# Retention's value and key projections moved from the middle stage's end to beside the sparse attention's lower half

## The chip, the core and the metric

The kernel runs on one core of a Trainium2 chip. The metric is the device time of one execution in microseconds (us). Matrix products run on TensorE (PE; its loads of weights are shown as PEld), the rest on VectorE (DVE), ScalarE (ACT) and GpSimd (POOL); SyncE (SP) issues nearly all transfers (DMAs). Each engine takes its instructions in the order in which the program has them, and waits at one until its inputs and its output buffer are ready.

## What is computed

One layer of a decoder over 1024 positions of width 1024: an RMS norm, one input projection into all the parts below, three groups of heads, a gate, one output projection with the residual, and a last RMS norm. Cut to what matters:

```python
u = rms_norm(h, attn_norm[layer])
proj = jnp.einsum('bsd,dc->bsc', u, w_in[layer])
(dq, dk, dv, sq, ckv, iq, ik, iw, rq, rk, rv, gate) = jnp.split(proj, split_points, axis=-1)
o_a = diff_attention(dq, dk, dv, ...)                        # 6 heads, dense causal, two maps each
o_b = dsa_attention(sq, rms_norm(ckv, ...), iq, ik, iw, ...) # 6 heads, the 256 best keys of each query
o_c = retention(rotary(rq, ...), rotary(rk, ...), rv, ...)   # 4 heads, chunks of 128 with a state
y = jax.nn.silu(gate) * jnp.concatenate([o_a, o_b, o_c], axis=-1)
h = h + jnp.einsum('bsc,cd->bsd', y, w_out[layer])
```

## The kernel before

Positions are worked in 8 blocks of 128. Float32 products of high precision are made of three matmuls, with each operand split into a high part and the small rest (`split`, L121): the names ending in `h` and `l`, as `wh` and `wl`, are these.

**Units of the input projection.** `gemm` (L269) makes one unit. The raw weights `wr` come from HBM through a ring of two buffers (`rtile`, L228) and are split by POOL into tiles `wh` and `wl` of a pool of five (`wsplit`, L242). A unit of retention (`rq`, `rk`, `rv`, 256 columns) has 8 tiles of 128 positions; each is 24 matmuls (L282 to L284) into a PSUM tile `pG`, of which there are two. `ret_evac` (L469) takes such a tile to SBUF: for `rv` one ACT copy (L479), for `rq` and `rk` two products on DVE (L491, L492) and three POOL instructions (L494 to L498). The result lies in a tile `rt` of a pool of three (`hl`) until its store to the DRAM array `rd` (L499), an SP transfer.

**Attention.** `attend` (L585) is used by both attentions. One step is one block of queries of one head: scores into PSUM `pS` (for the sparse one L720 and L721), scores with the mask to a tile `pp` with the row's maximum (DVE, L728), exponential (ACT, L729), normalization (DVE, L734 and L736), transposes into `pB` (L611), their copies to `pt` (ACT L113, or L115 where the scheduler may choose), and after each pair of blocks the product with the values `v` (L626). The sparse attention's lower half, `dsa(p, 0)`, takes blocks 0 to 3 against up to 512 keys, the upper half, `dsa(p, 1)`, blocks 4 to 7 against up to 1024; each has 3 pairs of heads, so 24 steps. Its output is multiplied with the gate (L758) and stored (L763).

**Stages.** `run` (L831) issues the work in stages. `interleave` (L58) draws from several generators and takes next the one whose issued cost, divided by its weight, is smallest. The middle stage mixes the dense attention, the selection of keys (`topk`, `ties`) and a list of projection units, `order` and the part of `order2` ahead of the bar, at weight `wg`. Then the values of the sparse attention are loaded (`v_load`, L811). The next stage mixes the sparse attention's lower half, the last `ties`, and, at weight `gw`, the units behind the bar followed by retention's first half with `out_weights` and the first part of block 7's output projection. The last mix is the sparse attention's upper half with retention's second half (blocks 4 to 7) and the output projection of two blocks. The output projection (`project`, L905) of the other blocks ends the program.

`out_weights` (L894) loads the output weights in 16 pieces through the same two `wr` buffers. For each of 8 row groups one piece is copied by ACT into `woh` (L113) with its rest `wol` by DVE (L123), the other is done by POOL alone (L119, L123). `woh` and `wol` take the place of the split input `uh` and `ul`, so the first waits for the last projection matmul.

The stages set the order in which instructions are issued to the framework. A scheduler then orders each engine's queue by its own timeline, so that instructions of neighbouring stages mix.

```python
interleave((seq(*(self.diff(p) for p in range(3))), K["wd"]),
           (seq(self.topk(), self.ties((3, 2))), K["wt"]),
           (units(K["order"] + " " + K["order2"].split("|")[0]), K["wg"]))
self.v_load()
interleave((seq(*(self.dsa(p, 0) for p in range(3))), 100), (self.ties((7, 6, 5, 4)), 110),
           (seq(units(K["order2"].split("|")[1]), mix((self.retention(0), K["rw"]),
                        (seq(self.out_weights(), self.project(K["pp"], 0)), K["ow"]))), K["gw"]))
```

Of the kernel before, what the change touches and what calls it, by code (L numbers as in the profile page):

```python
# [28 lines left out]
    0, 384, 768, 1152, 1536, 1664, 2176, 2248, 2504, 2760, 3016)  # L29
WA = 384 + 72  # L30
C_R = (C_RQ, C_RK, C_RV)
K = {'mk': 'up ky', 'mp': 's2 g5 g4', 'rt': ('hl', 'pq'), 's0': ('gg', 'gg', 'ag', 'gg', 'vg', 'gg', 'vg', 'vg'), 'xp': 2, 'bufs': (8, 3, 3, 5, 3, 4, 1), 'pp': (7,), 'rot': 0, 'order': 'g0 g1 k1 q1 k2', 'order2': 'q2 g2 rq g6 s0 ck g7 s1 M g3 rv rk | ', 'wd': 36, 'wt': 13, 'wg': 119, 'gw': 56, 'rw': 26, 'rx': 132, 'pw': 40, 'ow': 84, 'nf': 2, 'ev': 200, 'late': 8, 'de': ('aa', 'aa', 'aa'), 'da': 'ax', 'gd': (7, 4, 2), 'hlp': 'sqkk', 'tkp': '', 'vt': 'v', 'rs': 'x', 'nv': 1, 'dn': 'v', 'ws': 'gg', 'oe': ('av', 'gg'), 'one': 0, 'idx': (42, 40), 'iqs': 'iq2 iq3 q0 k0'}
NST, NP, NPQ, NW, NHL, NHALF, NY = K["bufs"]


# [33 lines left out]
class Trunk:  # L69
# [65 lines left out]
    def setup(self):  # L135
# [8 lines left out]
        for b in range(NB):  # L144
            self.x[b] = self.slot("x", [128, 1024])
            nc.sync.dma_start(self.x[b], i["x"][0, b * 128:(b + 1) * 128, :])
            if b == K["xp"] - 1:
                self.wide()
# [93 lines left out]
    def wsplit(self, c0, w):  # L242
        hs, ls = [], []
        if w == WA:
# [5 lines left out]
            for k in range(KC):  # L250
                self.split(hs[k], ls[k], self.dvw[k // 2][:, k % 2], *K["s0"][k])
            return hs, ls
        n = 1024 // w
        for k0 in range(0, KC, n):
            h, l = (self.wtile("w" + x, [n, w]) for x in "hl")
            for j in range(0, n, n // 2):
                raw = self.rtile([n // 2, w])
                self.nc.sync.dma_start(raw, self.i["w_in"][0, (k0 + j) * 128:(k0 + j + n // 2) * 128,
                                                           c0:c0 + w].rearrange("(k p) c -> p k c", p=128))
                self.split(h[:, j:j + n // 2], l[:, j:j + n // 2], raw, *K["ws"])  # L260
            hs += [h[:, j] for j in range(n)]
# [3 lines left out]
    def evict(self, evac, *args):  # L265
        with self.tc.high_priority(offset=K["ev"]):
            evac(*args)
# [21 lines left out]
    def to_dram(self, key, n=2):  # L289
# [3 lines left out]
        def evac(half, ps):  # L293
            sl = slice(half * 512, half * 512 + 512)
            t = self.sb.tile([128, 2, 512], FR, name=self.name("hl"), tag="hl", bufs=NHL)
            if key[:2] in K["hlp"]:
                nc = self.nc
# [682 lines left out]
```

## Time and profile before

| | |
|---|---|
| median of the runs shown | 781.14 us |
| the three runs | 777.98, 781.14, 785.86 us |
| the profiled execution | 785.29 us |
| its span, first to last instruction | 783.6 us |
| busy in the span: PE, DVE, ACT, POOL | 724.2, 551.5, 447.6, 311.5 us |
| mean granted clock of TensorE | 0.974 |
| moved by DMA | 113.05 MB |

Stretches of the trace are named by the time from the span's start. The span lies 1.7 us below the profiled execution's own time; that execution is 4.15 us slower than the median. Busy time of PE counts each matmul from its start to its modelled end, and matmuls overlap: how many fit is read from the distance between the starts. The idle time before an instruction, with what ended it, stands in brackets behind it; the name after the arrow is the engine, tile and line that was waited for. The granted clock is a share of full speed: 1.0 is the level of 2.4 GHz and 0.5 that of 1.2 GHz, and a value between them is a mean over a stretch with both.

### The profile page before, as it was taken

What the parts mean: (1) busy time and instruction counts of PE and PEld (TensorE: products, weight loads), DVE (VectorE), ACT (ScalarE), POOL (GpSimd) and SP (SyncE); (2) the same over time, 40 slices, a digit from 0 to 9 for tenths busy, and PEclk for the clock granted to TensorE, in tenths of its full rate; (3) what the DMA queues carried; (4) which work ended last, traced back from release to release, by engine and by line L of the source; (5) the groups of instructions that cost most, each with busy time, mean ns of one, the idle gap of its engine ahead of it and who ended that gap; (6) DMA issues with size and microseconds to landing.
All of it is one profiled execution on the core that took longest, in us unless ns stands there. A gap on an engine that the chain in (4) does not pass through costs nothing.

```text
span 783.6 us, 12891 instructions
## 1 busy us (share of the span) xinstructions
PE 724.2 (92%) x4314; PEld 597.4 (76%) x4314; DVE 551.5 (70%) x1312; ACT 447.6 (57%) x989; POOL 311.5 (40%) x343
## 2 busy tenths in 40 slices
PE   3999999999999999988799789998978999999996
PEld 3798888887887898766577567997855887787884
DVE  5920277789999989999889997325657766664443
ACT  4531255559888968787755566434356656554332
POOL 6401322225434438557347699335733242120000
PEclk9999999999999999999899999999968999999999
DMA  9303645454374352461274476564578974413351
GB/s 332 78 1 71 197 136 145 139 137 132 99 218 115 85 163 78 120 169 35 67 206 144 144 215 190 158 192 160 158 213 236 281 200 127 123 48 108 118 176 59
DMA packets 93250, 113.05 MB, mean 144 GB/s; under 512 B 11904, under 2 KB 63488, under 8 KB 93056
## 3 DMA queue, kind: packets, MB, share of 16 engines
q1 hardware_dynamic: 91888, 109.61, 48.1%
q10 hardware_dynamic: 1296, 2.62, 0.9%
q8 instruction: 34, 0.56, 0.3%
q14 instruction: 32, 0.26, 0.1%
HBM read 75.50 MB, written 36.18 MB: 143 GB/s over the span
## 4 chain that ended last, share of the span: by engine, by line
PE 61%; DVE 16%; DMA 6%; issue 6%; POOL 5%; ACT 4%; SPq 0%; DVEq 0%; POOLq 0%; ACTq 0%
PE pB L626 6%; PE pG L130 6%; PE pG L132 6%; PE pG L131 5%; PE pB L611 4%; PE pG L282 4%; PE pG L936 4%; PE pG L937 4%; PE pG L935 4%; PE pG L283 4%; PE pG L284 4%; DVE jv L378 3%; DMA wr<-in_w_in_dram 2%; PE pS L344 2%; PE pS L343 2%
## 5 line engine op out<-in xcount | busy, mean ns | idle before, releaser
L130 PE MATMUL pG<-uh,wh 128*128 128x512 f32 x352 | 141.6, 402 | 1.8 <-DVE gt L827 1.8
L132 PE MATMUL pG<-uh,wl 128*128 128x512 f32 x352 | 140.7, 400 | 0.6 <-POOL wl L123 0.6
L131 PE MATMUL pG<-ul,wh 128*128 128x512 f32 x352 | 139.4, 396 | 0.0
L123 POOL TENSOR_TENSOR wl<-wr,wh 128x512 fp32r<-128x512 f32 x56 | 79.3, 1430 | 106.3 <-PE pG L131 69.4
L392 ACT ACTIVATE ja<-sc,tk_c 128x896 int8<-128x896 f32 (+2 forms) x93 | 83.2, 895 | 17.3 <-DVE tk_c L399 12.0
L113 ACT ACTIVATE pt<-pB 128x512 f32<-128x512 f32 (+2 forms) x120 | 58.8, 496 | 43.8 <-PE pB L611 43.5
L130 PEld LDWEIGHTS pG<-uh,wh 128*128 128x128 f32 x352 | 66.8, 190 | 16.4 <-DVE gt L827 2.4
L132 PEld LDWEIGHTS pG<-uh,wl 128*128 128x128 f32 x352 | 66.4, 189 | 16.1 <-POOL wl L123 0.9
L611 PE MATMUL pB<-ident,pp 128*128 128x128 f32 x432 | 72.9, 287 | 5.5 <-DVE gt L758 3.4
L626 PE MATMUL pB<-pt,v 128*64 128x128 f32 x864 | 70.8, 302 | 7.6 <-ACT pt L113 7.0
L131 PEld LDWEIGHTS pG<-ul,wh 128*128 128x128 f32 x352 | 66.7, 189 | 13.0 <-issue 0.2
L626 PEld LDWEIGHTS pB<-pt,v 128*64 128x64 f32 x864 | 57.7, 147 | 18.9 <-ACT pt L113 9.5
L378 DVE TENSOR_SCALAR_CACHE_REDUCE jv<-sc,tk_c 128x640 bf16<-128x640 f32 (+4 forms) x81 | 69.2, 855 | 1.0
L611 PEld LDWEIGHTS pB<-ident,pp 128*128 128x128 f32 x432 | 51.2, 144 | 22.2 <-issue 9.1
L677 POOL TENSOR_SCALAR pq<-pq,mx 128x896 f32<-128x896 f32 (+7 forms) x48 | 43.2, 901 | 58.6 <-DVE mx L676 55.8
L119 POOL TENSOR_SCALAR wh<-wr 128x512 fp32r<-128x512 f32 x56 | 37.8, 680 | 59.9 <-DMA wr<-in_w_in_dram 54.3
L282 PE MATMUL pG<-wh,uh 128*128 128x256 f32 x192 | 55.0, 288 | 2.6 <-POOL wh L119 2.6
L283 PE MATMUL pG<-wl,uh 128*128 128x256 f32 x192 | 54.9, 286 | 0.0
L284 PE MATMUL pG<-wh,ul 128*128 128x256 f32 x192 | 54.3, 284 | 0.0
L346 ACT ACTIVATE pp<-pS 128x1024 f32<-128x1024 f32 (+5 forms) x48 | 36.5, 760 | 31.1 <-PE pS L344 31.0
L651 PE MATMUL pS<-st,st 128*128 128x512 f32 (+3 forms) x144 | 43.3, 368 | 11.5 <-DVE mx L662 8.9
L351 DVE SCALAR_TENSOR_TENSOR sc<-pp,iw,sc 128x1024 f32<-128x1024 f32 (+5 forms) x42 | 43.5, 1044 | 14.3 <-ACT pp L346 13.6
(218 smaller groups left out, 1756.1 us busy)
## 6 DMA issues: line engine op xcount, KB each, us to landing
wr<-in_w_in_dram SPq DMA_DIRECT2D x56, 256.0 KB, 3.2
st<-qdq SPq DMA_DIRECT2D x24, 256.0 KB, 4.2
st<-qkk SPq DMA_DIRECT2D x18, 256.0 KB, 5.9
x<-in_x_dram SPq DMA_DIRECT2D x8, 512.0 KB, 6.6
qiq<-hl SPq DMA_DIRECT2D x16, 256.0 KB, 3.5
st<-qiq SPq DMA_DIRECT2D x8, 512.0 KB, 3.3
wr<-in_w_out_dram SPq DMA_DIRECT2D x16, 256.0 KB, 3.4
xr<-in_x_dram SPq DMA_DIRECT2D x8, 512.0 KB, 3.5
```

The source lines that it names most:

```text
L113: self.nc.scalar.activation(out, in_, AF.Copy)
L123: (self.nc.vector if e2 == "v" else self.nc.gpsimd).tensor_tensor(lo, src, hi.bitcast(F), OP.subtract)
L130: mm(ps, wh, xh, start=start, stop=False)
L131: mm(ps, wh, xl, start=False, stop=False)
L132: mm(ps, wl, xh, start=False, stop=stop)
L282: mm(ps, uh, hs[k], start=k == 0, stop=False)
L283: mm(ps, uh, ls[k], start=False, stop=False)
L284: mm(ps, ul, hs[k], start=False, stop=k == KC - 1)
L378: nc.vector.tensor_scalar(jv[:, :nv[b]], hb if b == 7 and bit >= 16 else sc[b], t, 0.0, op0=op, op1=OP.add, accum_out=cnt[:, j:j + 1])
L392: nc.scalar.activation(ja[:, :nv[b]], sc[b], AF.Sign, bias=cut(b), scale=-1.0, accum_out=cnt[:, cols[b]:cols[b] + 1])
L611: nc.tensor.transpose(p[:, k], pr[:, (k0 + k) * 128:(k0 + k + 1) * 128], self.ident)
L626: self.last = nc.tensor.matmul(o[u * 64:(u + 1) * 64], vals[k], pts[g, a][:, k, u * 128:(u + 1) * 128], start=k == (i if u else 0), stop=k ...
```

## The change

Two entries of the table `K` that steers the program. The units `rv` and `rk` move behind the bar of `order2`, from the middle stage into the stage with the sparse attention's lower half; the weight `gw` of that stage's third stream rises from 56 to 97, which keeps about the former pace of issue for what follows the two units. The weights of the middle stage stay as they are.

```diff
-'order2': 'q2 g2 rq g6 s0 ck g7 s1 M g3 rv rk | '
+'order2': 'q2 g2 rq g6 s0 ck g7 s1 M g3 | rv rk'
...
-'gw': 56
+'gw': 97
```

No instruction is added or taken away. The orders of the engines are alike up to the first matmul of `rv`; `ties` keep their places on DVE, with other buffer numbers alone.

On PE, the sparse attention's first scores before: `pS900` is its first tile of scores, `pG847` and `pG851` are tiles of `rv`, `pB844` and `pB850` are values and transposes of the dense attention.

```order
L284 MATMUL pG847_4929<-wh813_4728,ul_106 128x256
L720 MATMUL pS900_5637<-st898_5631,st899_5632 128x384
L626 MATMUL pB844_4905<-pt833_4859,v46_294 64x128 x7
L611 MATMUL pB850_4958<-ident_70,pp837_4874 128x128
L282 MATMUL pG851_4966<-wh809_4718,uh_105 128x256
```

On PE, the sparse attention's first scores in the changed order: `pS852` is that first tile of scores, `pG882` and `pG915` are the second and the third tile of `rv`, `pB816` and `pB821` belong to the dense attention.

```order
L284 MATMUL pG882_5236<-wh862_5144,ul_106 128x256
L626 MATMUL pB816_4744<-pt803_4696,v46_294 64x128 x11
L611 MATMUL pB821_4771<-ident_70,pp808_4715 128x128 x3
L720 MATMUL pS852_5117<-st850_5111,st851_5112 128x384
L721 MATMUL pS852_5117<-st850_5111,st851_5112 128x384
L282 MATMUL pG915_5380<-wh858_5134,uh_105 128x256
```

The first scores stand behind the fourth tile of `rv` before, and behind the second now; before, the second half of them (L721) follows only behind the eighth.

On PE, from the last projection matmul on, before: `pG889` is the last tile of `rk`, `pS971`, `pS977` are scores, `pB956` and `pB963` values, the other `pB` transposes, all of the sparse attention's lower half.

```order
L284 MATMUL pG889_5371<-wh871_5128,ul_106 128x256
L626 MATMUL pB956_5839<-pt948_5812,v897_5629 64x128 x3
L611 MATMUL pB961_5863<-ident_70,pp951_5821 128x128
L720 MATMUL pS971_5903<-st966_5890,st967_5891 128x512
L721 MATMUL pS971_5903<-st966_5890,st967_5891 128x512
L720 MATMUL pS977_5922<-st966_5890,st967_5891 128x128
L721 MATMUL pS977_5922<-st966_5890,st967_5891 128x128
L611 MATMUL pB962_5868<-ident_70,pp955_5836 128x128 x2
L626 MATMUL pB963_5872<-pt960_5862,v897_5629 64x128 x3
L611 MATMUL pB979_5926<-ident_70,pp970_5900 128x128 x3
```

On PE, from the last projection matmul on, in the changed order: `pG1051` is the last tile of `rk`, `pS983` and `pS988` are scores, `pB970` values, the other `pB` transposes, and `pG1055` is retention's first block.

```order
L284 MATMUL pG1051_6180<-wh1033_5946,ul_106 128x256
L611 MATMUL pB967_5622<-ident_70,pp956_5566 128x128 x4
L720 MATMUL pS983_5713<-st978_5694,st979_5695 128x512
L721 MATMUL pS983_5713<-st978_5694,st979_5695 128x512
L626 MATMUL pB970_5634<-pt962_5604,v849_5109 64x128 x7
L611 MATMUL pB975_5663<-ident_70,pp965_5613 128x128
L720 MATMUL pS988_5735<-st978_5694,st979_5695 128x128
L721 MATMUL pS988_5735<-st978_5694,st979_5695 128x128
L611 MATMUL pB976_5671<-ident_70,pp969_5631 128x128 x2
L522 MATMUL pG1055_6217<-ident_70,rt1053_6214 128x128
```

Before, `pS971` is the tenth of the lower half's 24 score tiles, and scores of 15 steps stand behind the last projection matmul; now `pS983` is the eighteenth, and 7 stand behind it.

On ACT, from the seventh to the eighth copy of output weights, before: `woh` are the copies, `pp` exponentials of the sparse attention's upper half, `pt` copies of transposes, `yh` the split of block 7's projection input, `rt` retention's first block.

```order
L113 ACTIVATE woh_5720<-wr1024_6111 128x512
L113 ACTIVATE pt1076_6301<-pB1078_6310 128x2x128
L729 ACTIVATE pp1114_6517,mx1113_6516<-pp1114_6517,mx1113_6516 128x1024
L113 ACTIVATE yh1068_6264<-yr1066_6260 128x384
L729 ACTIVATE pp1126_6553,mx1125_6552<-pp1126_6553,mx1125_6552 128x640
L113 ACTIVATE pt1122_6538<-pB1123_6539 128x4x128
L115 COPY pt1122_6538<-pB1124_6545 128x3x128
L443 ACTIVATE rt907_5657<-rt907_5657 128x256
L444 ACTIVATE rt907_5657<-rt907_5657 128x256
L729 ACTIVATE pp1131_6579,mx1130_6578<-pp1131_6579,mx1130_6578 128x768
L113 ACTIVATE pt1122_6538<-pB1128_6564 128x4x128
L113 ACTIVATE woh_5720<-wr1053_6212 128x512
```

On ACT, from the sixth to the eighth copy, in the changed order, with the same names.

```order
L113 ACTIVATE woh_6224<-wr1068_6277 128x512
L113 ACTIVATE pt1140_6628<-pB1141_6629 128x4x128
L115 COPY pt1140_6628<-pB1142_6635 128x128
L113 ACTIVATE pt1140_6628<-pB1146_6649 128x4x128
L113 ACTIVATE woh_6224<-wr1070_6285 128x512
L115 COPY pt1140_6628<-pB1147_6655 128x2x128
L729 ACTIVATE pp1149_6662,mx1148_6661<-pp1149_6662,mx1148_6661 128x1024
L729 ACTIVATE pp1157_6715,mx1156_6714<-pp1157_6715,mx1156_6714 128x640
L113 ACTIVATE pt1153_6700<-pB1154_6701 128x4x128
L115 COPY pt1153_6700<-pB1155_6707 128x3x128
L113 ACTIVATE woh_6224<-wr1073_6300 128x512
```

Between the last two copies stood three exponentials of the upper half, and now two; between the sixth and the seventh stand none now. Counted over the whole queue, four exponentials of the upper half stood ahead of the eighth copy, and seven do now. The exponentials between successive copies, from the first to the eighth, are now 3, 2 and 3 of the lower half, then 2, 3, 0 and 2 of the upper.

## Rows read from the trace of the kernel before

**Rows 1.** The page, busy us (share of the span) and instructions of each engine.
```profile
PE 724.2 (92%) x4314; PEld 597.4 (76%) x4314; DVE 551.5 (70%) x1312; ACT 447.6 (57%) x989; POOL 311.5 (40%) x343
```

**Rows 2.** Stages: length; busy PE, PEld, DVE, ACT, POOL (count); clock; DMA share; GB/s.
```profile
484.00:559.50 75.50, 72.75 (x589) 66.52 (x589) 31.18 (x94) 27.85 (x74) 38.07 (x51) 1.00 0.54 167
559.50:609.30 49.80, 41.47 (x247) 29.97 (x247) 34.09 (x104) 27.93 (x72) 19.35 (x22) 0.83 0.79 221
609.30:724.70 115.40, 112.83 (x880) 91.70 (x878) 71.77 (x161) 65.72 (x142) 26.01 (x36) 1.00 0.49 144
724.70:783.60 58.90, 51.48 (x222) 41.80 (x222) 23.80 (x54) 17.60 (x42) 0.00 (x0) 0.97 0.34 118
```

**Rows 3.** PE in order of time, projection of retention: start, us, instruction.
```profile
523.22 0.28 PE L282 MATMUL pG<-wh,uh 128*128 128x256 f32 x1
523.34 0.28 PE L283 MATMUL pG<-wl,uh 128*128 128x256 f32 x1
```

**Rows 4.** PE in order of time, steps of the sparse attention between projections.
```profile
533.97 1.09 PE L626 MATMUL pB<-pt,v 128*64 128x128 f32 x14
534.99 0.33 PE L611 MATMUL pB<-ident,pp 128*128 128x128 f32 x1
...
539.18 0.65 PE L626 MATMUL pB<-pt,v 128*64 128x128 f32 x6
539.76 0.55 PE L611 MATMUL pB<-ident,pp 128*128 128x128 f32 x3
540.06 0.42 PE L720 MATMUL pS<-st,st 128*128 128x384 f32 x1
...
540.50 0.28 PE L282 MATMUL pG<-wh,uh 128*128 128x256 f32 x1
```

**Rows 5.** ACT in order of time, four of the eight copies of output weights.
```profile
572.84 0.63 ACT L113 ACTIVATE woh<-wr 128x512 fp32r<-128x512 f32 x1 [3.10 <-DMA wr<-in_w_out_dram]
...
578.01 0.63 ACT L113 ACTIVATE woh<-wr 128x512 fp32r<-128x512 f32 x1 [1.50 <-DMA wr<-in_w_out_dram]
...
597.69 0.62 ACT L113 ACTIVATE woh<-wr 128x512 fp32r<-128x512 f32 x1
...
609.33 0.63 ACT L113 ACTIVATE woh<-wr 128x512 fp32r<-128x512 f32 x1 [2.40 <-DMA wr<-in_w_out_dram]
```

**Rows 6.** Tile wr, 555 to 615 us: durations (ns, min/median/max), first and last start, waits.
```profile
L113 ACT ACTIVATE woh<-wr x8: 616/629/631, 559.4 to 609.3; 128x512 fp32r<-128x512 f32 x8
...
L123 DVE TENSOR_TENSOR wol<-wr,woh x8: 672/689/1540, 560.5 to 610.0; 128x512 fp32r<-128x512 f32 x8
...
  ACT woh L113: 7.0, 3
...
DMA to landing us min/median/max: 2.9/3.4/7.3
```

**Rows 7.** PE in order of time, the wait between the projections of values and keys.
```profile
532.00 0.51 PE L282 MATMUL pG<-wh,uh 128*128 128x256 f32 x2 [2.56 <-POOL wh L119]
```

**Rows 8.** ACT in order of time, first and fourth exponential of the upper half.
```profile
595.93 1.04 ACT L729 ACTIVATE pp<-pp,mx 128x896 f32<-128x896 f32 x1 [0.41 <-DVE mx L728]
...
605.41 0.94 ACT L729 ACTIVATE pp<-pp,mx 128x768 f32<-128x768 f32 x1
```

**Rows 9.** Two stretches of stage 2, columns as in rows 2.
```profile
573.40:594.90 21.50, 18.23 (x82) 12.44 (x82) 13.20 (x46) 11.58 (x33) 8.15 (x8) 0.60 0.72 206
594.90:602.50 7.60, 5.71 (x40) 4.06 (x40) 5.12 (x14) 4.68 (x11) 0.00 (x0) 1.00 0.86 254
```

**Rows 10.** PE in order of time, where the first of these stretches begins.
```profile
574.45 0.66 PE L611 MATMUL pB<-ident,pp 128*128 128x128 f32 x4 [3.38 <-DVE gt L758]
...
576.38 1.97 PE L626 MATMUL pB<-pt,v 128*64 128x128 f32 x14
```

**Rows 11.** PE in order of time, output projection alone.
```profile
724.94 0.39 PE L936 MATMUL pG<-wol,yh 128*128 128x512 f32 x1
725.17 0.40 PE L937 MATMUL pG<-woh,yr 128*128 128x512 f32 x1
```

More of the change, by code (lines that the diff above doesn't have):

```diff
@@ L31 @@
 C_R = (C_RQ, C_RK, C_RV)
-K = {'mk': 'up ky', 'mp': 's2 g5 g4', 'rt': ('hl', 'pq'), 's0': ('gg', 'gg', 'ag', 'gg', 'vg', 'gg', 'vg', 'vg'), 'xp': 2, 'bufs': (8, 3, 3, 5, 3, 4, 1), 'pp': (7,), 'rot': 0, 'order': 'g0 g1 k1 q1 k2', 'order2': 'q2 g2 rq g6 s0 ck g7 s1 M g3 rv rk | ', 'wd': 36, 'wt': 13, 'wg': 119, 'gw': 56, 'rw': 26, 'rx': 132, 'pw': 40, 'ow': 84, 'nf': 2, 'ev': 200, 'late': 8, 'de': ('aa', 'aa', 'aa'), 'da': 'ax', 'gd': (7, 4, 2), 'hlp': 'sqkk', 'tkp': '', 'vt': 'v', 'rs': 'x', 'nv': 1, 'dn': 'v', 'ws': 'gg', 'oe': ('av', 'gg'), 'one': 0, 'idx': (42, 40), 'iqs': 'iq2 iq3 q0 k0'}
+K = {'mk': 'up ky', 'mp': 's2 g5 g4', 'rt': ('hl', 'pq'), 's0': ('gg', 'gg', 'ag', 'gg', 'vg', 'gg', 'vg', 'vg'), 'xp': 2, 'bufs': (8, 3, 3, 5, 3, 4, 1), 'pp': (7,), 'rot': 0, 'order': 'g0 g1 k1 q1 k2', 'order2': 'q2 g2 rq g6 s0 ck g7 s1 M g3 | rv rk', 'wd': 36, 'wt': 13, 'wg': 119, 'gw': 97, 'rw': 26, 'rx': 132, 'pw': 40, 'ow': 84, 'nf': 2, 'ev': 200, 'late': 8, 'de': ('aa', 'aa', 'aa'), 'da': 'ax', 'gd': (7, 4, 2), 'hlp': 'sqkk', 'tkp': '', 'vt': 'v', 'rs': 'x', 'nv': 1, 'dn': 'v', 'ws': 'gg', 'oe': ('av', 'gg'), 'one': 0, 'idx': (42, 40), 'iqs': 'iq2 iq3 q0 k0'}
 NST, NP, NPQ, NW, NHL, NHALF, NY = K["bufs"]
```

## The prediction

> **What bounds the kernel now.** I read the page first, then the busy time by stages, then the instructions of TensorE (PE) and ScalarE (ACT) in order of time. The page has PE busy for 92% of the span [rows 1]; VectorE (DVE) follows at 70%. I cut the end of the kernel into four stages [rows 2]. Stage 1 (484.0 to 559.5 us) holds the projections of the retention's values and keys; stage 2 (559.5 to 609.3) begins with their last matmul and ends with the eighth and last ACT copy of the output weights; stage 3 (609.3 to 724.7) is the rest of the sparse attention's upper half with retention and output projection; stage 4 is output projection alone. Stages 1, 3 and 4 are PE's: busy 72.75 of 75.5, 112.83 of 115.4, and dense to the last projection matmul. Stage 2 is the weak one: PE 41.47 of 49.8 at a mean clock of 0.83, DVE 34.09, ACT 27.93. No engine fills it.
>
> How full PE is depends on the row that one trusts. By matmul busy time stage 2 has 8.3 us free. The loads of weights, PEld, are busy 29.97 us of it, which leaves 19.8 us [rows 2]. The Trainium skill (Perfetto Trace Analysis, Identifying the Most-Contended Engine) says that matmul busy time misjudges TensorE and that the share of weight loads should be used. The trace agrees that busy time flatters: a projection matmul is shown with 0.28 us, but the next starts 0.12 us later [rows 3]. By that rule the most the sum below could reach is -19.8 us, by busy time -8.3.
>
> What sets the length of stage 2? The output weights come through two buffers `wr`, one split by ACT and DVE, one by GpSimd (POOL). The eight ACT copies `woh` start from 559.4 to 609.3, 49.9 us, so 7.1 us apart on the mean [rows 6]. The shortest distance is 5.17 (572.84 to 578.01 [rows 5]). A load lands 2.9 to 7.3 us after its issue, median 3.4 [rows 6]; with a copy (0.63) and DVE's subtraction (0.69) behind it, that is a ring of 4.7 us before SP's issue. ACT takes its queue in order: while it waits for a load [3.10 us at 572.84, rows 5], the attention's exponentials behind it wait too.
>
> **The change part by part.** The same instructions are issued; the 16 retention tiles (24 matmuls, each 0.12 us behind the last, 2.9 us a tile [rows 3]) keep their place in PE's order. What moves is the sparse attention's lower half, 24 steps of one query block each. Counted in the orders, the scores of 15 steps stand behind the last projection matmul before, and of 7 now; transposes and values of 18 before, of 11 now.
>
> Stage 1 grows by the scores of eight steps and the rest of seven. Per head (four steps) the value matmuls take 1.02 us (14 of them) and 0.58 (6), three transposes 0.30, so ten 1.0, and the two score matmuls of 384 columns 0.44, so 2 x 1280 columns 1.47 [rows 4]; so a step costs 0.37 for its scores and 0.65 for the rest, and 8 x 0.37 + 7 x 0.65 = **+7.5 us**. Their exponentials (ACT) and reductions (DVE) lie beside matmuls: DVE has 31.18 busy of 75.5 in this stage [rows 2], and a step comes about every 24 projection matmuls.
>
> Between value and key projections PE waits 2.56 us for the next weights [rows 7], since a weight buffer comes free only behind the last value tile. In the new order value matmuls, transposes and scores of two steps stand in that gap; bounds are 0 and -2.6, I take half, **-1.3**.
>
> SP's queue: the stores of retention tiles now stand among more loads and stores of the attention. A tile has three buffers, each due again after three tiles, so 8.6 us of matmuls alone; loads here land in 2.9 to 7.3 us [rows 6]. I cost this at nothing, at worst +5 (five key tiles, 1 us each). The value array's load of the sparse attention keeps its place behind the last dense attention output.
>
> Stage 2 holds less work, but the ring of output weights is the same. In ACT's new order the exponentials between successive `woh` copies are, for the seven distances, 3, 2 and 3 of the lower half, then 2, 3, 0 and 2 of the upper. A lower step takes 2.36 us in before's bare stretch (559.5 to 594.9 for 15, bounds of rows 2 and 9). An upper step takes 3.16 (595.93 to 605.41 in three distances [rows 8]). I give a distance the larger of its steps and 5.3, little above the shortest seen: 7.1, 5.3, 7.1, 6.3, 9.5, 5.3, 6.3 = 46.9. Stage 2: 46.9 - 49.9 = **-3.0 us**. Bounds: seven times 5.17 = 36.2 gives -13.7; a ring as slow as in the last distance of before (597.69 to 609.33 is 11.6 [rows 5]) in two of seven places gives about 56, +6.
>
> Stage 3 and 4: at the last copy, ACT has done seven exponentials of the upper half, before four. So three upper steps leave stage 3. PE alone needs (26 values x 0.073 per two steps, 6.5 transposes, 2 x 832 columns, at the unit times of rows 4) 2.5 us, the bare row is 3.16; I take 2.8, as stage 3 is fuller: -8.4. The first part of block 7's projection (18 matmuls, 0.23 us apart [rows 11]) moves into it: +4.2. Projections of blocks 1 and 2 (96 matmuls, 22 us) move behind the last attention step, at the same spacing: nothing. Together **-4.2**. What this takes away is filler between the upper half's steps; retention's blocks stay as such.
>
> Sum: 7.5 - 1.3 - 3.0 - 4.2 = -1.0 us on an execution of 785.3. That execution lies 4.2 above the median of the runs shown, 781.14, whose spread is 7.9. Set off from the median, the forecast is **780 us: no change**. About 1%, 7.8 us, is what a measurement of this kernel can tell from none.
>
> **The rivals.** *Faster: the bare stage shrinks with its work.* If the distances of stage 2 were set by the attention's chain, and the ring ran at its best, stage 2 would take 36.2 us, and the sum is -1.0 - 10.7 = -11.7, so 769.5. For it speaks that ACT waited for `wr` only 7.0 us in all of stage 2 [rows 6]; against it, that one distance in the new order holds no exponential at all and can be no shorter than the ring. The Trainium skill (Perfetto Trace Analysis, Optimization Strategy) advises to interleave stretches that are limited by different engines, which is what this does; by it the faster case is the expected one.
>
> *Slower: the clock falls where upper steps now stand.* After 3.38 us of idle PE [rows 10] the granted clock was 0.60 on the mean from 573.4 to 594.9 [rows 9], mostly the 1.2 GHz level, and 14 value matmuls took 1.97 us against 1.09 [rows 4, 10]. Before, small lower steps filled that stretch. Now the last lower steps end some 18 us into the bare stage and upper ones follow with no filler. At 2.5 us of PE work each, an upper step would take 4.5 at half clock instead of 3.16; seven of them +9.4, so the sum is +8.4 and the time 789.5. It decides if PE idles early in the bare stage as it did before 574.45, behind an ACT queue that waits for `wr`. Against it: upper steps use PE more, and at 594.9 the clock came back as they began [rows 9]. The Trainium skill (TensorE: Matmul & The Clock Gate, HAM oscillation) describes such falls when matmuls wait for DMA; by it this rival is the likelier the longer the bare stage is.
>
> *Retention's stores stuck in SP's queue* behind the attention's: +5, so 785, still within 1%.
>
> **How the numbers follow.** No change within 1%: 0.50 (the stuck stores lie in it). Faster: 0.28, mostly the shrinking stage. Slower: 0.22, mostly the clock, and stalls of the denser order that no row shows. The range reaches to both rivals, 768 to 791.
>
> **What would show it.** The last projection matmul some 6 us later than 559.5, and the wait for weights of 2.56 us halved; the eight `woh` copies over some 47 us (36 for the first rival, 56 with a clock of about 0.6 for the second); the last value matmul of attention about 22 us earlier than before, and 73 us of dense projection behind it, now of blocks 1 to 7. The step most likely wrong is the length of stage 2. A stage 1 longer by over 14 us would mean that stores or loads hold the projections.

## The result and the profile after the change

The change makes the kernel slower by 0.8%: the median of 20 runs is 789.60 us against 783.75 us of 20 runs of the kernel before, ratio 1.0081 with a 95% interval of 1.0060 to 1.0102. The forecast was no change, 780 us, a step of -1.0 us; the step came out at +5.85. The change lies inside the 1% that the prediction took for the limit of what can be told from none, yet 20 runs of each kernel set it clear of none. Of the 9.6 us between 780 and 789.60, 2.6 are the base: the forecast was set off from the median of three runs, 781.14.

The page of the changed kernel shows busy times that answer to [rows 1] almost to the microsecond: the work is the same.

```profile
PE 722.2 (92%) x4314; PEld 597.4 (76%) x4314; DVE 552.5 (70%) x1312; ACT 447.6 (57%) x989; POOL 314.1 (40%) x343
```

The profiled execution takes 786.32 us (span 784.6). That is 3.3 below the median, and the profiled execution of before (785.29) lies 1.5 above its own, so this pair shows 1.0 of the 5.85 us. The stages, cut at the same events and with the columns of [rows 2]: end of the last projection matmul, eighth ACT copy of output weights, last value matmul of attention.

```profile
484.00:565.00 81.00, 79.07 (x652) 72.67 (x651) 40.15 (x123) 34.55 (x95) 38.20 (x50) 1.00 0.58 177
565.00:612.10 47.10, 37.71 (x262) 28.07 (x260) 31.03 (x84) 26.45 (x62) 16.52 (x18) 0.89 0.72 202
612.10:700.90 88.80, 83.85 (x688) 68.41 (x689) 56.12 (x130) 52.66 (x115) 26.06 (x34) 0.98 0.53 158
700.90:784.60 83.70, 75.93 (x332) 61.03 (x332) 34.43 (x74) 25.04 (x59) 3.93 (x7) 0.98 0.33 110
```

Stage 1 is longer by 5.5 us (81.0 against 75.5), stage 2 shorter by 2.7 (47.1 against 49.8), stages 3 and 4 together shorter by 1.8 (172.5 against 174.3). The tail alone grew from 58.9 to 83.7.

Another cut says more. In TensorE's and ACT's instructions in order of time, its events are the last projection matmul (`L284`), the first exponential of the attention's upper half (`L729`), TensorE's one long wait, and the first matmul of the output projection (`L935`). TensorE, changed kernel:

```profile
564.70 0.28 PE L284 MATMUL pG<-wh,ul 128*128 128x256 f32 x1
...
614.63 3.57 PE L626 MATMUL pB<-pt,v 128*64 128x128 f32 x30 [3.46 <-ACT pt L115]
618.13 0.66 PE L611 MATMUL pB<-ident,pp 128*128 128x128 f32 x4
618.54 0.47 PE L935 MATMUL pG<-woh,yh 128*128 128x512 f32 x1
```

ACT, changed kernel:

```profile
588.17 1.03 ACT L729 ACTIVATE pp<-pp,mx 128x896 f32<-128x896 f32 x1
...
612.07 0.63 ACT L113 ACTIVATE woh<-wr 128x512 fp32r<-128x512 f32 x1 [3.71 <-DMA wr<-in_w_out_dram]
...
617.04 0.52 ACT L113 ACTIVATE yh<-yr 128x384 fp32r<-128x384 f32 x1 [1.44 <-issue]
```

The first projection matmul in the kernel before, to set beside its first upper exponential at 595.93 [rows 8]:

```profile
602.55 0.50 PE L935 MATMUL pG<-woh,yh 128*128 128x512 f32 x1 [1.44 <-ACT yh L113]
```

Before, the output projection starts 6.6 us behind the first upper exponential (602.55 - 595.93), after three steps of the upper half. Now it starts 30.4 us behind (618.54 - 588.17), after nine. The lower half does end sooner, 23.2 us behind the last projection matmul (588.17 - 564.98) against 36.4. But from the first upper exponential to the end it takes 196.4 us (784.6 - 588.17) against 187.7 (783.6 - 595.93). Busy times in the two stretches, the changed kernel first, then the one before:

```profile
588.00:618.50 30.50, 23.20 (x166) 18.20 (x167) 19.37 (x45) 18.57 (x38) 9.90 (x10) 0.89 0.76 228
```

```profile
595.90:602.55 6.65, 4.75 (x38) 3.39 (x36) 4.14 (x13) 4.13 (x9) 0.00 (x0) 1.00 0.93 271
```

TensorE is free for 7.3 us of the first (30.50 - 23.20) and for 1.9 us of the second.

What is the first projection late for? A candidate stands in SP's queue. In the changed kernel, the end of the 16 loads `wr` of output weights (`L901`), and behind them the input `yr` of block 7's projection (`L920`):

```profile
596.19 8.69 SPq L901 DMA_DIRECT2D wr<-in_w_out_dram  x3
...
609.57 0.34 SPq L901 DMA_DIRECT2D wr<-in_w_out_dram  x1
609.95 0.45 SPq L912 DMA_DIRECT2D fn<-in_final_norm_dram  x1
610.44 0.43 SPq L920 DMA_DIRECT2D yr<-yd  x1
```

In the kernel before:

```profile
595.54 0.58 SPq L912 DMA_DIRECT2D fn<-in_final_norm_dram  x1
596.17 0.44 SPq L920 DMA_DIRECT2D yr<-yd  x1
596.71 0.43 SPq L901 DMA_DIRECT2D wr<-in_w_out_dram  x1
...
606.81 0.34 SPq L901 DMA_DIRECT2D wr<-in_w_out_dram  x1
```

`yr` stood behind 13 of the 16 loads; now it stands behind all of them. A load waits at the head of the queue for one of the ring's two buffers, and what is behind it waits too: below, the load at 604.56 goes out as POOL has done with a piece (603.23 + 1.31 = 604.54). The profile's chain of waits of the changed kernel runs through these pieces (start, us, what):

```profile
596.19 6.26 DMA wr<-in_w_out_dram
602.53 0.63 POOL woh L119
603.23 1.31 POOL wol L123
604.56 2.89 DMA wr<-in_w_out_dram
...
609.57 0.34 SPq L901
609.95 0.45 SPq L912
610.44 2.75 DMA yr<-yd
613.19 0.91 ACT pp L729 x2
614.10 0.48 ACT pt L115
614.63 3.57 PE pB L626 x30
```

The step behind `yr` can't be taken at its word: it leads to exponentials, which read no `yr`, and that load landed 6.5 us behind its issue, not 2.75. TensorE's wait of 3.46 us is for `pt`, which ACT copied behind its own wait of 3.71 us for the last `wr`. The first projection matmul itself shows no wait: `yh` was ready at 617.56 (617.04 + 0.52), and TensorE, which takes its queue in order, came to the projection at 618.54, behind the nine steps that stand ahead of it there. So this execution shows ring, `yr` and projection one behind the other, and leaves open which of them holds TensorE.

### The profile page after: what moved, and what is told of

Read it like the earlier page. It is cut to its first block, busy times and chain, and to the rows that moved or that the text cites. A ratio compares the mean times of both kernels' runs of the same rounds, so it can differ in the third digit from the quotient of the medians.

```text
span 784.6 us, 12890 instructions
## 1 busy us (share of the span) xinstructions
PE 722.2 (92%) x4314; PEld 597.4 (76%) x4314; DVE 552.5 (70%) x1312; ACT 447.6 (57%) x989; POOL 314.1 (40%) x343
## 4 chain that ended last, share of the span: by engine, by line
PE 59%; DVE 12%; DMA 12%; POOL 5%; issue 5%; ACT 4%; SPq 2%; DVEq 0%; ACTq 0%; POOLq 0%
PE pG L130 7%; PE pG L132 7%; PE pG L131 7%; PE pB L626 5%; PE pG L937 4%; PE pG L936 4%; PE pG L935 4%; PE pB L611 3%; PE pG L282 3%; PE pG L283 3%; PE pG L284 3%; PE pS L344 2%; PE pS L343 2%; DMA yo<-yo 2%; DMA wr<-in_w_in_dram 2%
## 5 line engine op out<-in xcount | busy, mean ns | idle before, releaser
L123 POOL TENSOR_TENSOR wl<-wr,wh 128x512 fp32r<-128x512 f32 x56 | 81.3, 1464 | 105.9 <-PE pG L131 70.9
L611 PE MATMUL pB<-ident,pp 128*128 128x128 f32 x432 | 71.2, 283 | 3.6 <-DVE gt L758 3.1
L651 PE MATMUL pS<-st,st 128*128 128x512 f32 (+3 forms) x144 | 44.9, 379 | 11.2 <-DVE mx L662 7.3
L284 PE MATMUL pG<-wh,ul 128*128 128x256 f32 x192 | 54.5, 285 | 0.0
L346 ACT ACTIVATE pp<-pS 128x1024 f32<-128x1024 f32 (+5 forms) x48 | 36.5, 759 | 31.1 <-PE pS L344 30.5
```

What stands on the lines that cost most here:

```text
L123: (self.nc.vector if e2 == "v" else self.nc.gpsimd).tensor_tensor(lo, src, hi.bitcast(F), OP.subtract)
L284: mm(ps, ul, hs[k], start=False, stop=k == KC - 1)
L611: nc.tensor.transpose(p[:, k], pr[:, (k0 + k) * 128:(k0 + k + 1) * 128], self.ident)
```

## The experiments

The theories, in the order in which they arose. *Ring*: the two buffers fix the length of the bare stage, whatever work it holds. *Clock*: the added time is half clock behind idle gaps. *First stage*: attention steps among projections cost more than I gave. *Filler*: the projections of blocks 1 and 2 are missed between the upper half's steps. *ACT's queue*: ACT's wait for the eighth copy holds what TensorE needs. *SP's queue*: the first projection's input stands behind the whole ring. Each ratio is to the kernel before, timed on the same chip in the same rounds.

**Both kernels once more.** No edit.

> The kernel before, once more, for a second profile and the noise of the comparison. All theories: ratio 1.000, within 0.3%. By the theory of the clock (the added time is stretches at half clock behind idle gaps of TensorE in the bare stage and after it), the stretches below clock 0.9 in the last 225 us sum to about 30 us here and to more in the changed kernel. By the theory of the first stage (attention steps among the projections cost more than the 0.37 and 0.65 us that I gave them) the clock is alike in both, and the last projection matmul ends near 559.5 us here and later than 567 there.

> The changed kernel once more, since its first profiled execution lies 3.3 us below its median and shows only 1.0 us of the 5.9. Ratio 1.006 to 1.010 to before. Theory of the clock: the last projection matmul again near 565, the eighth copy of output weights near 612, and the excess lies behind it, with idle gaps of over 2 us and clock below 0.9 in 565 to 625 us. Theory of the first stage: the excess lies ahead of 570 us.

Measured: 1.0016 (0.9987 to 1.0045) and 1.0094 (1.0056 to 1.0132). The mean granted clock over the runs of the two kernels on this chip is the same, 0.9745 in 31 runs of the kernel before and 0.9746 in 8 of the changed one, at 782.3 and 789.2 us: the clock theory falls. With the second profiles there are two executions of each. From the end of the last matmul of the gate unit `g3` (493.97 and 489.95 before, 493.67 and 492.61 now) I get, before and now:

| stretch, us | before | changed | difference of means |
|---|---|---|---|
| to the last projection matmul's end | 65.5, 64.0 | 71.3, 72.0 | +6.9 |
| from there to the first upper exponential | 36.4, 32.8 | 23.2, 23.4 | -11.3 |
| from there to the end of the span | 187.7, 187.5 | 196.4, 197.0 | +9.1 |

Sum +4.7, of 5.85 timed (6.9 on this chip). The first stage grew about as I had reckoned (+6.2), so that theory falls as well. (Of all runs below, seven of the changed kernel and eight of the kernel before have the same order on TensorE up to the last projection matmul; their means are 72.0 and 64.4, 7.5 apart.) The upper half takes back most of what the lower half gained. Stage 2 in the second profile of before is 46.1 long, where the first had 49.8; in that of the changed kernel it is 47.9:

```profile
553.90:600.00 46.10, 38.02 (x247) 27.49 (x247) 33.68 (x104) 27.92 (x73) 19.68 (x22) 0.93 0.82 239
```

```profile
564.60:612.50 47.90, 37.78 (x263) 28.32 (x261) 31.39 (x84) 26.50 (x62) 16.16 (x18) 0.89 0.68 202
```

**The ring relaxed**, in both kernels:

```diff
-                raw = self.rtile([512])
+                raw = self.wtile("wr", [512], F) if c.start else self.rtile([512])
```

The second piece of each row group (`c.start` not 0), which GpSimd splits, takes a buffer of the pool of five; the first stays in the ring.

> The changed kernel with the pieces of the output weights that GpSimd splits no longer in the ring of two buffers wr but in the pool of split weights, which is free by then. Nothing is left out. Theory of the ring (the bare stage holds less work now, but the ring keeps it as long, 47 us): the eight ACT copies come over 36 us or less in place of 47, ACT waits for loads under 2 us of the 7.7, and the time falls by 4 to 10 us against the changed kernel, to about 780 to 785. Rival (the bare stage is set by the attention's chain of DVE, ACT and PE, so the ring only takes free time): the copies come earlier, the time stays within 2 us of the changed kernel.

> The kernel before with the same edit of the ring. Theory of the ring: with more attention work in the bare stage the ring costs less here, so the gain is 0 to 4 us, smaller than in the changed kernel, and the two kernels then stand within 2 us or in the opposite order. Rival (attention's chain): unchanged within 2 us, ratio 0.998 to 1.002, and the changed kernel with the edit is still 4 to 8 us slower than this.

Measured: 0.9931 (0.9903 to 0.9958), 776.4 us, and 0.9959 (0.9932 to 0.9986), 778.8 us. The changed kernel gains 12.8 us (789.2 to 776.4), more than the 4 to 10 expected, and the kernel before 3.5. By their medians the order of the two turns round; the intervals overlap, so that they differ at all is not shown. The first projection matmul now comes 0.5 us behind the first upper exponential, and from that to the end it takes 186.4 us (779.7 - 593.28):

```profile
593.28 1.04 ACT L729 ACTIVATE pp<-pp,mx 128x896 f32<-128x896 f32 x1 [0.31 <-DVE mx L728]
```

```profile
593.77 0.48 PE L935 MATMUL pG<-woh,yh 128*128 128x512 f32 x1
```

The loss hangs on the ring. But the edit does several things: weights earlier, next to no wait for them in ACT's queue (0.5 us in place of 7.7), `yr` sooner, and 162 projection matmuls ahead of the last value matmul instead of 66. It beats both kernels.

**The filler, taken from before and given to the changed kernel**:

```diff
-'nf': 2
+'nf': 1
...
-        drain(self.project(range(K["nf"], 3)))
         with self.tc.issue_after(self.last.ins):
-            drain(self.project([3]))
+            drain(self.project(range(K["nf"], 4)))
```

> The kernel before with one thing of the changed order: the output projections of blocks 1 and 2 (96 matmuls, 22 us) behind the sparse attention's last step, no longer between the steps of its upper half. All up to the first projection of block 0 stays. Theory of the filler (the upper half's steps stall by the same amount with or without these matmuls between them, so in the tail they are paid in full): the last value matmul comes only some 17 us earlier, and the time rises by 4 to 7 us against the kernel before, to 786.5 to 789.5; that is most of the change's loss. Theory of the ring alone, and my prediction's step (moving them costs nothing): within 1.5 us of the kernel before.

```diff
-'pw': 40
+'pw': 60
```

> The changed kernel with the projections back: the weight of retention's second half and the projection in the last mix 60 instead of 40, by which the projections of blocks 0 to 2 stand among the upper half's steps again, 162 matmuls ahead of the last value matmul as in the kernel before, in place of 66. All up to the eighth copy of output weights stays as in the changed kernel. Theory of the filler: faster than the changed kernel by 4 to 7 us, 782 to 785, so not slower than before. Theory of the ring alone: within 1.5 us of the changed kernel, 788 to 790.5.

Measured: 1.0024 (0.9997 to 1.0051) without the filler: 1.9 us, not clear of none and 4 at the interval's end, where 4 to 7 were expected. With the filler given back it is 1.0157 (1.0118 to 1.0196), a miss of the whole theory: 796.5 us, slower still. The weight moves retention's second half too, and its blocks then stand by themselves; TensorE waits in them at 645 to 651 us, and the granted clock falls, from 1.00 in the 20 us ahead to 0.83:

```profile
645.37 0.71 PE L531 MATMUL pG<-rt 64*128 64x128 f32 x8 [0.73 <-ACT rt L524]
...
647.43 0.71 PE L537 MATMUL pG<-rt 128*128 128x128 f32 x4 [1.34 <-DVE rt L533]
...
651.39 1.22 PE L441 MATMUL pG<-rt,bd 128*128 128x256 f32 x2 [0.92 <-ACT rt L440]
```

```profile
640.00:660.00 20.00, 16.78 (x94) 12.20 (x93) 8.30 (x17) 6.45 (x16) 7.21 (x11) 0.83 0.61 173
```

**The change by half**: `'... M g3 rv | rk'`, `'gw': 76`.

> The change by half: only the keys' projection moves behind the bar, with the third stream's weight at 76. Scores of 9 steps stand behind the last projection matmul (15 before, 7 in the changed kernel), and the projections of blocks 1 and 2 stand in the tail as in the changed kernel. Theory of the filler: most of the loss is there already, 787 to 790. Rival (the loss is in proportion to the attention moved into the first stage, or to the stall at the eighth copy): 785 to 788, between the two kernels.

Measured: 1.0044 (1.0019 to 1.0069). By its median (788.4) it lies with the filler theory, by its ratio half way. Its first projection comes 30.3 us behind the first upper exponential (619.34 - 589.03), as late as in the whole change, with 4.1 us of growth in the first stage instead of 6.9, and from that exponential to the end it takes 196.6 us, as long as in the whole change. The run tells nothing apart.

**ACT's wait taken away**, for the last row group, then for all:

```diff
-                self.split(self.woh[:, k, c], self.wol[:, k, c], raw, *e)
+                self.split(self.woh[:, k, c], self.wol[:, k, c], raw, *("gg" if k == KC - 1 else e))
```

> The changed kernel with both pieces of the last row group of output weights split by GpSimd, so that ACT's eighth copy and its wait for the load are gone from ACT's queue; the rest of the order is nearly untouched. Theory of the queue (ACT waits 3.65 us for the last load, ahead of a transpose's copy for which TensorE then idles 3.4 us): that idle gap near 612 us goes to under 1 us and the time falls by 3 to 5 us against the changed kernel, to 784.5 to 787. Theory of the late weights (TensorE lacks the projection, and it makes no difference whose queue waits): within 1.5 us of the changed kernel.

> The kernel before with the same edit. Its eighth copy waits 2.4 us, but TensorE idles only 1.0 to 1.4 us there. Theory of the queue: 0 to 2 us faster than the kernel before. Theory of the late weights: within 1 us.

```diff
-'oe': ('av', 'gg')
+'oe': ('gg', 'gg')
```

> The changed kernel with all 16 pieces of output weights split by GpSimd, through the same two buffers: neither ACT's nor DVE's queue holds a wait for a load any more, and ACT and DVE have 5 us less work each. Theory of the queue: the lower half ends sooner and the time falls by 4 to 9 us against the changed kernel, to 780.5 to 785.5. Theory of the late weights: GpSimd takes at least 16 x 1.9 = 30 us and the ring still has two buffers, the first projection matmul comes no earlier than 55 us behind the last matmul of the keys, and the time stays within 1.5 us of the changed kernel.

> The kernel before with the same edit. Theory of the queue: 2 to 4 us faster than the kernel before (as much as with the ring relaxed, 3.5), less than the changed kernel gains. Theory of the late weights: within 1.5 us, or slower where GpSimd becomes the later one.

Measured: 1.0058 (1.0029 to 1.0086) and 0.9962 (0.9932 to 0.9992) for the last row group; 1.0120 (1.0079 to 1.0161) and 0.9932 (0.9901 to 0.9963) for all. Freed of the same waits, the kernel before gains 3 us and 5, more than either theory gave it. The changed one gains nothing that is clear of none: with the last row group alone its interval overlaps the unedited one's, and with all on GpSimd it is slower by 2 to 3 us, if by anything. In the changed kernel the wait comes back under another name. With the last row group on GpSimd TensorE waits 3.21 us for `yh`, the split of `yr`:

```profile
617.84 0.79 PE L935 MATMUL pG<-woh,yh 128*128 128x512 f32 x1 [3.21 <-ACT yh L113]
```

With all on GpSimd it waits 7.86 us. ACT waits for the load, and SP had that behind three loads `wr` that took 6.51 us to issue:

```profile
623.62 0.77 PE L935 MATMUL pG<-woh,yh 128*128 128x512 f32 x1 [7.86 <-ACT yh L113]
```

```profile
622.95 0.52 ACT L113 ACTIVATE yh<-yr 128x384 fp32r<-128x384 f32 x1 [8.34 <-DMA yr<-yd]
```

```profile
610.36 6.51 SPq L901 DMA_DIRECT2D wr<-in_w_out_dram  x3
616.91 0.42 SPq L912 DMA_DIRECT2D fn<-in_final_norm_dram  x1
617.39 0.42 SPq L920 DMA_DIRECT2D yr<-yd  x1
```

So ACT's wait for weights is not what the changed kernel loses by. Late weights and SP's queue remain. The kernel before with all pieces on GpSimd is as fast as the changed one with the relaxed ring (0.9932 and 0.9931): the best time here doesn't need the move.

**Weights early, filler absent**: the relaxed ring with the edit of the missing filler.

> The changed kernel with the relaxed ring of output weights, and with the projections of blocks 1 and 2 kept in the tail as in the changed kernel (66 projection matmuls ahead of the last value matmul, 318 behind). It parts the two things that the relaxed ring did at once: weights earlier, and the projections back among the upper half's steps. Theory of the late weights (the loss is the stretch of 30 us and nine upper steps between the upper half's first exponential and the first projection matmul): that stretch stays under 5 us, and the time is 1 to 4 us above the relaxed ring alone, 777.5 to 781, still faster than before. Theory of the filler: the gain goes with the projections' place, 785 to 789.

Measured: 0.9943 (0.9922 to 0.9964), 777.2 us, within 1 us of the relaxed ring alone by the ratios. With the relaxed ring the place of the projections of blocks 1 and 2 is worth next to nothing.

**The ring halved**, in both kernels: one buffer for all 16 pieces.

```diff
+        raw = self.rtile([512])
         for k in range(KC):
             for c, e in zip((slice(0, 512), slice(512, D)), K["oe"]):
-                raw = self.rtile([512])
```

> The kernel before with the suspected cost doubled: one buffer for all 16 pieces of output weights instead of two. Nothing is left out. Theory of the late weights: the last piece is split 15 us or more later than the 53 us behind the last projection matmul, the upper half waits for it or runs ahead without projections, and the time rises by 8 to 20 us, to 792 to 804. Theory that the added time came from the first stage or the clock: within 3 us of the kernel before.

> The changed kernel with the same edit. The order puts the first projection matmul behind the scores of 45 of 48 steps. Theory of the late weights: the distance to the kernel before with the same edit grows beyond the 6 us between the two as they are (with the relaxed ring it was -2.4): 8 us or more, so 802 to 825. Rival (the distance of 6 us is the first stage's growth, whatever the weights): it stays at 4 to 8 us.

Measured: 1.0073 (1.0048 to 1.0098), 786.9 us, less than the 792 expected, and 1.0391 (1.0372 to 1.0410), 812.0 us. The distance between the kernels, which the move of two units alone makes, is -2.4 us with the relaxed ring, 5.9 with two buffers, 25.1 with one. The first stage's growth can't do that. But the last weights are late in both (split 96 us behind the last projection matmul in the kernel before, 82 in the changed one), and the one loses 5.7 us by it, the other 24 (from a ratio of 1.0081). In the kernel before, `yr` stands behind 6 loads, in the changed one behind all 16 and is issued at 645.08:

```profile
644.61 0.42 SPq L912 DMA_DIRECT2D fn<-in_final_norm_dram  x1
645.08 0.43 SPq L920 DMA_DIRECT2D yr<-yd  x1
```

```profile
651.22 0.79 PE L935 MATMUL pG<-woh,yh 128*128 128x512 f32 x1 [6.32 <-ACT yh L113]
```

**The first projection moved ahead, its load with it**; ring, buffers and engines stay: the generator of output weights is drawn for three row groups, then the first part of block 7's projection is issued, then the other five. Its matmuls move ahead on TensorE too, and the projections of blocks 1 and 2 come back among the upper half's steps (162 projection matmuls ahead of the last value matmul, 66 in the changed kernel).

```diff
-(seq(self.out_weights(), self.project(K["pp"], 0)), K["ow"])
+(self.wo7(), K["ow"])
...
+    def wo7(self):
+        w = self.out_weights()
+        for _ in range(3):
+            yield next(w)
+        yield from self.project(K["pp"], 0)
+        yield from w
```

> The changed kernel with the first part of block 7's projection issued behind three row groups of output weights (all that it uses) and ahead of the other five. In SP's queue its input load yr then stands behind 6 of the 16 loads wr instead of behind all 16; ring, buffers and engines stay. Theory of SP's queue (what is late is not the last piece of the weights but the first projection, whose input load stands behind the whole ring): the stretch from the upper half's first exponential to the first projection matmul falls from 30 us to under 5, and the time falls by 6 to 12 us against the changed kernel, to 776 to 783. Theory of the late weights (what counts is the last piece, 53 us behind the last projection matmul): within 2 us of the changed kernel, 786.5 to 790.

> The kernel before with the same edit. There yr stands behind 13 of the 16 loads and the first projection matmul comes 6.5 us behind the upper half's first exponential already. Theory of SP's queue: little to gain, 0 to 4 us faster, and the changed kernel with the edit comes within 3 us of it on either side. Theory of the late weights: both stay where they are, 6 us apart.

Measured: 0.9970 (0.9938 to 1.0002), 779.7 us, and 1.0020 (0.9993 to 1.0047), 784.2 us. The changed kernel gains 9 us (from a ratio of 1.0081 and 1.0094), the kernel before nothing, and the changed one is now the faster by its median, by 4.5 us where at most 3 were expected. In the kernel before, the edit puts `yr` behind 4 loads and the first projection matmul 27.5 us ahead of the first upper exponential. In the changed kernel `yr` is issued at 577.72, behind 6 loads, and the first projection matmul comes 0.8 us ahead of the first upper exponential:

```profile
575.84 1.36 SPq L901 DMA_DIRECT2D wr<-in_w_out_dram  x2
577.24 0.43 SPq L912 DMA_DIRECT2D fn<-in_final_norm_dram  x1
577.72 0.43 SPq L920 DMA_DIRECT2D yr<-yd  x1
```

```profile
585.10 0.49 PE L935 MATMUL pG<-woh,yh 128*128 128x512 f32 x1 [1.53 <-ACT yh L113]
```

```profile
588.00:618.00 30.00, 28.47 (x218) 22.60 (x216) 24.31 (x50) 18.33 (x41) 14.04 (x16) 0.96 0.80 243
```

In the stretch where TensorE was busy for 23.20 of 30.50 us it is now busy for 28.47 of 30.00. Yet the output weights come later than in the changed kernel: their last piece is split 60 us behind the last projection matmul, not 53. So it is not the last piece that counts, but how early the projection is issued and can start. Whether the one load held it or its place in TensorE's order, this edit can't part, since it moves both.

Seen together, eleven of the kernels, each from its profiled execution (first upper exponential by `L729`, first projection matmul by `L935`, end of span):

| kernel | loads `wr` ahead of `yr` | exponential to projection, us | steps in it | exponential to end, us | ratio |
|---|---|---|---|---|---|
| relaxed ring, changed | 14 | 0.5 | 1 | 186.4 | 0.9931 |
| before | 13 | 6.6 | 3 | 187.7 | 1 |
| projection ahead, changed | 6 | -0.8 | 0 | 192.5 | 0.9970 |
| projection ahead, before | 4 | -27.5 | 0 | 186.5 | 1.0020 |
| relaxed ring, before | 16 | 4.8 | 2 | 187.1 | 0.9959 |
| GpSimd alone, before | 12 | 9.7 | 3 | 189.9 | 0.9932 |
| one buffer, before | 6 | 6.9 | 1 | 199.5 | 1.0073 |
| half the change | 16 | 30.3 | 9 | 196.6 | 1.0044 |
| changed | 16 | 30.4 | 9 | 196.4 | 1.0081 |
| GpSimd alone, changed | 16 | 37.2 | 11 | 203.4 | 1.0120 |
| one buffer, changed | 16 | 63.5 | 19 | 222.2 | 1.0391 |

The place in the queue costs as much as the ring ahead of it is slow: behind 16 loads of the relaxed ring `yr` is early enough. And an early start is not all: with one buffer the kernel before starts the projection in time and still loses 5.7 us (that the later row groups hold its matmuls is my reading, not tested), and a start 27.5 us ahead gains it nothing.

## Why the prediction was wrong

**Stage 1, +7.5 - 1.3 = +6.2.** Near: +6.9 from two executions of each kernel, +7.5 from the fifteen with these orders. The wait for weights of 2.56 us [rows 7] is gone, but TensorE waits 1.52 us there for something else, a norm of the dense attention's output.

**Retention's stores in SP's queue, nothing.** Right for the stores: TensorE waits for none of them in this stage. But the prediction costed nothing else in SP's queue, and there `yr` had come to stand behind the last `wr`. Retention's first load stood worse too: it was issued 2.4 us behind the last projection matmul (567.36 - 564.98), where it went out 0.4 us ahead of it before (559.07 against 559.51), and TensorE waits for it in stage 2, in both executions, where it did not before:

```profile
571.01 0.48 PE L522 MATMUL pG<-ident,rt 128*128 128x128 f32 x1 [2.78 <-DMA rt<-rd]
```

**Stage 2, -3.0.** The sum of 46.9 us was right (47.1 and 47.9), its parts were not, which is luck: the seven distances were 8.1, 7.3, 7.3, 4.1, 7.9, 4.4 and 8.1 against 7.1, 5.3, 7.1, 6.3, 9.5, 5.3 and 6.3. The 5.3 that I took for the ring's pace was undercut twice, and where no exponential stood between two copies they came 4.4 apart:

```profile
599.62 0.63 ACT L113 ACTIVATE woh<-wr 128x512 fp32r<-128x512 f32 x1 [0.68 <-DMA wr<-in_w_out_dram]
603.97 0.63 ACT L113 ACTIVATE woh<-wr 128x512 fp32r<-128x512 f32 x1 [1.04 <-DMA wr<-in_w_out_dram]
```

The difference was wrong: one execution of before gave 49.8, the next 46.1, so that it is -0.5 on the mean (a third execution with the same order up to there has 49.9, in the run without the filler, and 48.9 for the changed order, in the run with the weight at 60). The stage did keep its length, and the faster rival (36 us) did not come.

**Stages 3 and 4, -4.2.** They came 1.8 us shorter in both pairs (172.5, against 174.3 and 174.2). I let three upper steps leave stage 3 at 2.8 us each and the first part of block 7's projection enter, and took the rest as filled as before.

**The step that failed** is thus the credit of 7.2 us (-3.0 and -4.2) behind the last projection matmul for the steps that had left: 2.2 us of it came (36.4 + 187.7 and 32.8 + 187.5 us before, 23.2 + 196.4 and 23.4 + 197.0 now), and that miss of 5.0 is nearly the whole step of 5.85. What I left out is that the stretch would not stay filled: the projection began only when the ring was through. Cut at the first upper exponential, the lower half gave 11.3 us and the upper half took back 9.1. Nine of its steps ran without projection matmuls at 3.4 us each (30.4 / 9) instead of three, with TensorE free for 7.3 us of them. With the projection issued ahead the same stretch, from the last projection matmul to the end, takes 214.1 us (21.6 + 192.5), 8.1 less than the mean of before: about the credit forecast, from one execution.

**Blocks 1 and 2's projections in the tail, nothing.** Right as far as the runs tell: 1 us with the relaxed ring, 2 in the kernel before, neither clear of none. The tail is 83.7 us rather than 73; the last value matmul ends 23.8 us earlier (700.9 against 724.7), near the 22 forecast.

**The slower rival** named 789.5, and 789.6 was measured: luck, not its mechanism, and the base was 2.6 us off. It wanted the clock down; the granted clock of stage 2 was 0.89 in both executions against 0.83 and 0.93, and over the runs the same. The Trainium skill (TensorE: Matmul & The Clock Gate, HAM oscillation) has matmuls that wait for DMA lose their clock. The trace shows a little of it: 0.89 in the 30.5 us above, and 0.51 from 614.6 to 618.0 us, behind the wait of 3.46 us for `pt`, where 30 value matmuls took 3.57 us. No run here charges the loss to it. The Trainium skill (Perfetto Trace Analysis, Optimization Strategy) has it that interleaving stretches with different limits may help, which spoke for a gain. The runs give one only where the projection is not late: by the medians of the two kernels -2.4 us with the relaxed ring and -4.5 with the projection ahead.

**Stuck stores, +5.** The right queue and the wrong transfers: what came late in it were loads, retention's first and the output projection's.

**What stays open.** The profiled executions account for 4.7 of 5.85 us. Why half the change costs about half, though its projection starts as late, is not settled. The run that moved the projection ahead gains 9 us by its time, and its profile shows 5 of them behind `g3`. Whether the load `yr` or the projection's place in TensorE's order does it stays open: no run moved the load alone, or issued it from another engine's queue.

## What to carry to other kernels

When work is moved ahead of a fixed chain of transfers, ask what the engine will do when the moved work has run out and the chain has not. Read the order of the issuing queue as closely as that of the bound engine: a small load behind a ring of loads that wait for buffers is issued when the ring is through (here at 610.44 us, behind all 16). Cut the stages at the same step of the work in both kernels, not at the transfer that both wait for. And take the length of a stage from several executions before a difference of a few us is drawn from it.

## What the runs showed of the hardware

The first 490 us scatter by themselves. The last matmul of `g3` ends at 489.8 us in one profiled execution (the changed kernel with the weight at 60) and at 498.0 in another (with the relaxed ring), with the same order on TensorE up to there; that is more than the change's whole effect, so one profile of each kernel could not show it. Loads `wr` that wait for a buffer hold SP's queue for 8.69 us at one place and 6.51 at another, and the cost of that is not in the loads' own rows: TensorE's idle times of 3 to 8 us stand behind them.
